# A macaron decoder block on one core: the third product ahead of two turns at the start, and the last norm's weights multiplied on GpSimd at the end

## The chip, the cores and the metric

The kernel runs on one core of one Trainium2 chip. The metric is the device time of one execution in microseconds, the median of several runs. In the rows of the profile PE is TensorE (PEld its weight loads), DVE is VectorE, ACT is ScalarE, POOL is GpSimd and SP is SyncE, which issues most DMAs.

## What is computed

One decoder block on x of 1024 tokens by 1024 channels in float32:

```
h = x + 0.5 * swiglu(rms(x, g1), w1a, w3a, w2a)      # first half-step, 2816 wide
u = rms(h, g_mix)
h = h + (sigmoid(gA) * yA + sigmoid(gB) * yB) @ W_o   # attention and pooling mixers on u
h = h + 0.5 * swiglu(rms(h, g2), w1b, w3b, w2b)      # second half-step
out = rms(h, g_final)
```

with `rms(x, g) = x / sqrt(mean(x*x) + eps) * g` and `swiglu(x, w1, w3, w2) = (silu(x @ w1) * (x @ w3)) @ w2`. The change touches the entry into the first half-step and the last norm.

## The kernel before

**Products.** Every large matrix product is cut into two by two blocks and done with seven block products in place of eight, by sums and differences of the blocks. To keep float32's accuracy with fast matmuls each operand is split into a high and a low part (`hi` and `lo`): ScalarE rounds a copy to the high part, VectorE or GpSimd subtracts it from the source for the low part, and TensorE adds up high by high, high by low and low by high. One product of a 128-wide block of weights with half the tokens (512) is thus 12 matmuls of 128x128 by 128x512 (`Sevens.product`, L316); its weights are split by ScalarE (L304, tile `wc`) and by GpSimd or VectorE (L307).

**The entry into the first half-step** (`begin_up1`, L877, an order written out by hand). The rows of x come by DMA in eight tiles of 128 tokens. TensorE runs twelve idle matmuls of ones first (`keep_on(12)`, L905), and then turns the norm's weights into a row (`gains`, L896, copied by VectorE at L912). For each tile ScalarE squares and sums (`squares`, L259), VectorE forms the mean and GpSimd takes the power (`inverse`, L263 and L264), VectorE scales half a row (L270), and TensorE turns it, 128x128 at a time, by a matmul with the identity (L392: "the turn" of a tile). ScalarE copies the turned tile as the high part (`Rows`, L393), VectorE forms the low part (`lower`, L396), and ScalarE later keeps the turned tile in h (`keep`, L400).

The low channels of tiles 0 to 3 are block b11, their high channels block b21. Products 0 to 3 of the entry multiply b11 with the first four blocks of weights (a and b of pairs 0 and 1: `u_f10a`, `u_f10b`, `u_f11a`, `u_f11b`); product 4 (`u_f10a` again) is the first that reads b21. The order on TensorE before is: product 0, turns of the high channels of tiles 0 and 1, product 1, turns of tiles 2 and 3, product 2, product 3, product 4, the turns of tile 4 (b22, then p12 by L457, then the difference t3 that GpSimd forms at L441, tile `s_f1t`), product 5, and so on (`Entry.run`, L433 on). Below, the first product is product 0, and so the third is product 2 and the fifth is product 4. ScalarE has, in this order: high parts of tiles 2 and 3, the copy of product 1 (L576), the square of tile 5, four `keep`s (L400), the operand of product 4 (L304, `wc_f10a`), the copy of product 2, the operand of product 5.

**The end.** The last products add 0.5 * (gate @ w2) into h: seven block products (`DOWN`, L97) of six steps each (`Down`, L707). A step's operands are prepared two steps ahead (`begin`): VectorE sums two blocks of weights (L766, tile `s_f2w`), ScalarE makes the high parts (L746, `bhi` and `ahi`), VectorE or GpSimd the low parts (L750, `blo` and `alo`). When a block product is complete its four banks are added into the tiles of h by VectorE (`add`, L793), and `after2(m, t)` (L2193) is called for the tile. Tiles 0 to 3 are complete after the fifth block product; their norm goes in one piece. Of tiles 4 to 7 the low channels are complete after the sixth and the high channels after the seventh:

- after the sixth, `low_half(t)` (L2154): ScalarE squares the low half and sums (L2157), writing the squares into the output tile; for tile 7 VectorE also multiplies the low halves of tiles 5 and 6 by the norm's weights (`with_gain`, L2165).
- after the seventh, `high_half(t)` (L2169), `power(t)` (VectorE L2173, GpSimd L2174), and one tile later `send_out(t)`: VectorE scales the high half by the power and the weights in one operation (L2179) and SyncE sends it; ScalarE scales the low half, which has its weights already, in place (L2183) and sends it. Tile 4's low half goes another way: `send_low(4)`, one operation of VectorE (L2189) from h, sent by SyncE.

For this last block product the last two steps are done together, tile by tile: nine matmuls for tile 4, its add and `after2`, then nine for tile 5, and so on. The operations of each engine run in the order in which the program issues them.

Of the kernel before, what the change touches and what calls it, by code (L numbers as in the profile page):

```python
# [12 lines left out]
AF = mybir.ActivationFunctionType  # L13
OP = mybir.AluOpType
AX = mybir.AxisListType

P = 128
# [109 lines left out]
def tile_block(  # L127
# [28 lines left out]
    nc = tc.nc  # L156
    ve, ac, gp, pe = nc.vector, nc.scalar, nc.gpsimd, nc.tensor
# [10 lines left out]
    def bank(tag, name):  # L168
        return psum.tile([P, HALF], F32, tag=tag, name=name)
# [18 lines left out]
    h = []  # L188
# [77 lines left out]
    def scaled(t, out, gain):  # L266
        ve.scalar_tensor_tensor(out, h[t], inv.pop(t)[:, 1:2], gain, op0=OP.mult, op1=OP.mult)
# [15 lines left out]
    LOWS, HIGHS = slice(0, HALF), slice(HALF, S)  # L283
# [575 lines left out]
    def load_all():  # L859
        load_rows(0, 1, 2, 3)  # L860
        raws.depth = 2
        raws.load()
        load_rows(4)
        raws.depth = 3
        raws.load()
        load_rows(5)
        raws.depth = 4
        raws.load()
        load_rows(6, 7)
        raws.depth = 6  # L870
        raws.load()
# [5 lines left out]
    def begin_up1():  # L877


        load_all()  # L880
        idle = bank("mm", "idle")

        def keep_on(n):

            for _ in range(n):
                pe.matmul(idle[:, :P], ones, ones, start=True, stop=True)

        def widen(b):
            k = slice(4 * b, 4 * b + 4)
            ve.tensor_copy(columns[:, k], gain1[:, k, None].to_broadcast([P, 4, P]))  # L890

        def gains(b):

            p = bank("acc", f"gain{b}")
            for k in range(4):
                pe.transpose(p[:, k * P:(k + 1) * P], columns[:, 4 * b + k], ident)  # L896
            return p

        r = {}

        def rows(t, what, c, tag="acc"):
            scaled_part(t, c, gain_row)
            r[t] = Rows(X, what, h[t][:, c], t, tag)

        keep_on(12)  # L905
        widen(0)
        squares(0, square)
        widen(1)
        inverse(0)
        g = [gains(b) for b in range(2)]  # L910
        keep_on(2)
        ve.tensor_copy(gain_row[:, LOWS], g[0])  # L912
        for t in range(1, 4):
            squares(t, square)
        inverse(1)
        rows(0, "b11", LOWS)
        keep_on(2)
        rows(1, "b11", LOWS)
        inverse(2)
        inverse(3)  # L920
        keep_on(2)
        pairs = [Pair(sv1, j, sums, True, j == 2) for j in range(3)]
        entry = pre_run(sv1, [(q, m) for m in (1, 2) for q in pairs[:2]] + [(pairs[2], m) for m in (1, 2)],
                        pairs[0], h[:4])
        entry.operand(0)
        rows(2, "b11", LOWS)
        keep_on(3)
        rows(3, "b11", LOWS, "mm")
        keep_on(2)
        ac.activation(gain_row[:, HIGHS], g[1], AF.Copy)  # L930
        for t in range(4):
            r[t].lower()
        sv1.terms = (0, 2, 1)
        entry.product(0)
        sv1.terms = (0, 1, 2)
        entry.operand(1)
        for t in range(4):
            r[t].keep(h[t][:, LOWS])

        square2 = columns_tile  # L940
        squares(4, square2)
        for t in (0, 1):
            rows(t, "b21", HIGHS)
        entry.product(1)
        entry.out(0)
        entry.operand(2)
        entry.operand(3)
        inverse(4)
        r[0].lower()
        for t in (2, 3):  # L950
            rows(t, "b21", HIGHS)
            r[t - 1].lower()
        entry.product(2)
        entry.out(1)
        squares(5, square2)
        r[3].lower()
        for t in range(4):
            r[t].keep(h[t][:, HIGHS])
        entry.product(3)
        entry.operand(4)  # L960
        entry.out(2)
        entry.operand(5)
        entry.out(3)

        def high(t, part):
            if part == 0:
                inverse(t)
                return
            scaled(t, h[t], gain_row)
            return h[t]  # L970

        def after(t):
            if t + 2 < NT:
                squares(t + 2, square2)
            if t < 6:
                raws.depth = t + 3
                raws.load()

        entry.run(high, after, 4)
        return pairs  # L980
# [304 lines left out]
    def mix_operand(k, part=0):  # L1285
        if k < len(items):
# [5 lines left out]
            else:  # L1292
# [3 lines left out]
    entry = Entry(svm, [(q.quad, m, q.out) for j in (0, 2) for m in (1, 2) for q in mixes[j:j + 2]], h[:4],  # L1296
                  mix_operand)
# [443 lines left out]
    ends = []  # L1741
# [175 lines left out]
    op = wo.enter_context(sbuf("ops", "right"))  # L1917
# [102 lines left out]
    with tc.manual_schedule():  # L2020
# [28 lines left out]
        for i in range(2, STEPS - 4):  # L2049
            step_o(i)  # L2050
            m, st = i // 2 - 1, i % 2
# [95 lines left out]
    final_gain = gains_of[1]  # L2147
# [4 lines left out]
    ends = {}  # L2152

    def low_half(t):  # L2154

        y, st = h_tile(f"n4_{t}"), small.tile([P, 4], F32, tag="nlast", name=f"nst_last{t}")
        ac.activation(y[:, LOWS], h[t][:, LOWS], AF.Square, scale=D ** -0.5, accum_out=st[:, 0:1])  # L2157
        ends[t] = y, st
        if t == 7:
            with_gain(5)  # L2160
            with_gain(6)

    def with_gain(t):
        y = ends[t][0]
        ve.tensor_tensor(y[:, LOWS], h[t][:, LOWS], final_gain[:, LOWS], op=OP.mult)  # L2165

    def high_half(t):
        y, st = ends[t]
# [7 lines left out]
    def send_out(t):  # L2176
        y, st = ends[t]
        rows = slice(t * P, (t + 1) * P)
        ve.scalar_tensor_tensor(y[:, HIGHS], h[t][:, HIGHS], st[:, 3:4], final_gain[:, HIGHS],  # L2179
                                op0=OP.mult, op1=OP.mult)  # L2180
        nc.sync.dma_start(out[rows, HIGHS], y[:, HIGHS])
        if t > 4:
            ac.activation(y[:, LOWS], y[:, LOWS], AF.Copy, scale=st[:, 3:4])  # L2183
            nc.scalar.dma_start(out[rows, LOWS], y[:, LOWS])

    def send_low(t):
        y, st = ends[t]
        rows = slice(t * P, (t + 1) * P)
        ve.scalar_tensor_tensor(y[:, LOWS], h[t][:, LOWS], st[:, 3:4], final_gain[:, LOWS],  # L2189
                                op0=OP.mult, op1=OP.mult)  # L2190
        nc.sync.dma_start(out[rows, LOWS], y[:, LOWS])

    def after2(m, t):  # L2193
        if m == len(DOWN) - 3:
            rows = slice(t * P, (t + 1) * P)
            nc.sync.dma_start(out[rows, :], norm_rows(t, final_gain, "n4", own_row))
        elif m == len(DOWN) - 2:
            low_half(4 + t)
        elif m == len(DOWN) - 1:
            high_half(4 + t)  # L2200
            if t > 0:
                send_out(3 + t)
            power(4 + t)
            if t == 0:
                with_gain(7)
            elif t == 1:
                send_low(4)
            elif t == 3:
                send_out(7)

    with sbuf("steps2", "right") as pool:
# [95 lines left out]
```

## Time and profile before

| | us |
|---|---|
| median of 3 runs (lowest, highest) | 1906.85 (1904.89, 1909.58) |
| the profiled execution | 1908.91 |
| its span, first to last instruction | 1907.0 |
| TensorE busy in it | 1888.8 |
| VectorE busy | 1328.2 |
| ScalarE busy | 774.4 |
| GpSimd busy | 713.7 |

All times in the rows are of the profiled execution, counted from the start of its span. A timeline row gives the start, the duration, the engine, the line, the operation, its tiles (output, arrow, inputs), its shape and a count where equal operations in a row are put together; in brackets stands how long the engine was idle before it and who ended that. A matmul's duration is longer than the distance to the next one, because matmuls overlap; the distance is what it costs. Releasers are inferred, and where several were waited for the name can be wrong.

### The profile page before, as it was taken

What the parts mean: (1) busy time and instruction counts of PE and PEld (TensorE: products, weight loads), DVE (VectorE), ACT (ScalarE), POOL (GpSimd) and SP (SyncE); (2) the same over time, 40 slices, a digit from 0 to 9 for tenths busy, and PEclk for the clock granted to TensorE, in tenths of its full rate; (3) what the DMA queues carried; (4) which work ended last, traced back from release to release, by engine and by line L of the source; (5) the groups of instructions that cost most, each with busy time, mean ns of one, the idle gap of its engine ahead of it and who ended that gap; (6) DMA issues with size and microseconds to landing.
All of it is one profiled execution on the core that took longest, in us unless ns stands there. A gap on an engine that the chain in (4) does not pass through costs nothing. (4 is left out here: it accounts for less than half of the span.)

```text
span 1907.0 us, 24693 instructions
## 1 busy us (share of the span) xinstructions
PE 1888.8 (99%) x8822; PEld 1564.4 (82%) x8822; DVE 1328.2 (70%) x1975; ACT 774.4 (41%) x1394; POOL 713.7 (37%) x533
## 2 busy tenths in 40 slices
PE   9999999999999999999999999999999999999998
PEld 8888888888878888888888788888888888888886
DVE  6876556558677777658886787787665566577777
ACT  7423333333335543334445762363333333333344
POOL 4433333331222354445544366543333333312131
PEclk9999999999999999999999999999999999999999
DMA  4154223336466626765578867644433223454564
GB/s 189 59 198 163 83 89 120 124 116 220 135 212 219 204 89 218 240 219 188 211 253 317 283 221 275 255 157 139 157 122 116 83 94 121 140 199 133 198 216 166
DMA packets 144020, 330.78 MB, mean 173 GB/s; under 512 B 17561, under 2 KB 39065, under 8 KB 142361
## 3 DMA queue, kind: packets, MB, share of 16 engines
q1 hardware_dynamic: 140152, 318.36, 48.2%
q10 hardware_dynamic: 3744, 10.85, 1.6%
q8 instruction: 69, 1.13, 0.2%
q14 instruction: 55, 0.44, 0.1%
HBM read 229.61 MB, written 99.55 MB: 173 GB/s over the span
## 5 line engine op out<-in xcount | busy, mean ns | idle before, releaser
L788 PE MATMUL d_f<-bhi_f,alo_f 128*128 128x512 f32 x616 | 240.3, 390 | 1.9 <-POOL alo_f L750 1.4
L788 PE MATMUL d_f<-bhi_f,ahi_f 128*128 128x512 f32 x616 | 240.4, 390 | 0.6 <-ACT h L400 0.4
L788 PE MATMUL d_f<-blo_f,ahi_f 128*128 128x512 f32 x616 | 239.7, 389 | 0.0
L750 POOL TENSOR_TENSOR alo_f<-g_f,ahi_f 128x512 fp32r<-128x512 f32 x60 | 83.4, 1407 | 276.0 <-ACT ahi_f L746 276.0
L316 PE MATMUL u_mixm<-xhi_t_mix,wc_mixm 128*128 128x512 f32 x608 | 157.7, 391 | 0.2 <-ACT wc_mixm L304 0.2
L788 PEld LDWEIGHTS d_f<-bhi_f,alo_f 128*128 128x128 f32 x616 | 115.6, 188 | 27.7 <-POOL alo_f L750 2.9
L788 PEld LDWEIGHTS d_f<-bhi_f,ahi_f 128*128 128x128 f32 x616 | 115.6, 188 | 25.1 <-ACT h L400 0.9
L788 PEld LDWEIGHTS d_f<-blo_f,ahi_f 128*128 128x128 f32 x616 | 115.6, 188 | 24.0
L316 PEld LDWEIGHTS u_mixm<-xhi_t_mix,wc_mixm 128*128 128x128 f32 x608 | 113.4, 188 | 24.1 <-ACT wc_mixm L304 0.7
L316 PE MATMUL u_mixm<-xhi_b_mix,wc_mixm 128*128 128x512 f32 x456 | 120.4, 392 | 0.5 <-DVE y_m L1068 0.5
L307 POOL TENSOR_TENSOR wc_mixm<-s_mixm,wc_mixm 128x512 fp32r<-128x512 f32 x52 | 78.0, 1501 | 110.3 <-ACT wc_mixm L304 96.2
L316 PEld LDWEIGHTS u_mixm<-xhi_b_mix,wc_mixm 128*128 128x128 f32 x456 | 84.8, 188 | 18.1 <-issue 0.9
L304 ACT ACTIVATE wc_mixm<-s_mixm 128x512 fp32r<-128x512 f32 x76 | 47.1, 629 | 110.4 <-DVE s_mixm L358 53.6
L746 ACT ACTIVATE ahi_f<-g_f 128x1024 fp32r<-128x1024 f32 x84 | 82.0, 976 | 3.6 <-DMA g_f<-gs_f 3.6
L316 PE MATMUL u_mixm<-xlo_t_mix,wc_mixm 128*128 128x512 f32 x304 | 81.3, 389 | 0.0
L307 POOL TENSOR_TENSOR wc_mixm<-raw,wc_mixm 128x512 fp32r<-128x512 f32 x40 | 59.3, 1484 | 43.1 <-ACT wc_mixm L304 32.4
L1988 PE MATMUL wo<-w_o,o_hi 128*128 128x512 f32 x224 | 69.5, 391 | 0.3 <-DVE merge L1803 0.3
L746 ACT ACTIVATE bhi_f<-s_f2w 128x512 fp32r<-128x512 f32 x55 | 32.7, 628 | 87.1 <-DVE s_f2w L766 79.4
L746 ACT ACTIVATE bhi_f<-s_f1w 128x512 fp32r<-128x512 f32 x55 | 32.7, 629 | 86.2 <-DVE s_f1w L766 72.2
L316 PEld LDWEIGHTS u_mixm<-xlo_t_mix,wc_mixm 128*128 128x128 f32 x304 | 57.1, 188 | 12.0
L750 DVE TENSOR_TENSOR alo_f<-g_f,ahi_f 128x1024 fp32r<-128x1024 f32 (+1 forms) x48 | 57.6, 1200 | 7.4 <-ACT ahi_f L746 7.4
L316 PE MATMUL u_mixm<-xlo_b_mix,wc_mixm 128*128 128x512 f32 x228 | 61.0, 389 | 0.0
(1332 smaller groups left out, 4758.6 us busy)
## 6 DMA issues: line engine op xcount, KB each, us to landing
g_f<-gs_f SPq DMA_DIRECT2D x70, 512.0 KB
gs_f<-y_f SPq DMA_DIRECT2D x88, 256.0 KB
raw<-in_w2a_dram SPq DMA_DIRECT2D x35, 512.0 KB
raw<-in_w2b_dram SPq DMA_DIRECT2D x35, 512.0 KB
gs_f<-gb_f SPq DMA_DIRECT2D x46, 256.0 KB
raw<-in_w1a_dram SPq DMA_DIRECT2D x22, 512.0 KB
raw<-in_w3a_dram SPq DMA_DIRECT2D x22, 512.0 KB
raw<-in_w1b_dram SPq DMA_DIRECT2D x22, 512.0 KB
```

Source lines behind the costliest of these rows:

```text
L304: ac.activation(w[:, 0], src, AF.Copy)
L307: eng.tensor_tensor(w[:, 1], src, w[:, 0].bitcast(F32), op=OP.subtract)
L316: pe.matmul(p, a, b, start=(start and n == 0), stop=(n == 11), skip_group_check=not start)
L746: ac.activation(hi[:, c], src, AF.Copy)
L750: eng.tensor_tensor(lo[:, d], src[:, o], hi[:, d].bitcast(F32), op=OP.subtract)
L788: pe.matmul(self.banks[m][t], l, r, start=(first and q == 0), stop=(last and q == 2))
L1988: pe.matmul(banks[m][t], l, r, start=(st == 0 and j == 0 and q == 0), stop=(st == 1 and j == 1 and q == 2))
```

## The change

Three edits. At the start the first run of idle matmuls has nine instead of twelve. Product 2 of the entry is issued ahead of the scaled rows, turns and low parts of tiles 2 and 3's high channels, directly behind product 1; the orders of VectorE, ScalarE, GpSimd and SyncE at this place stay as they were. At the end the low halves of all of tiles 4 to 7 are multiplied by the norm's weights on GpSimd, each directly behind its square, instead of tiles 5 to 7 on VectorE later; and ScalarE scales all four, so that `send_low` is gone. Tile 4's low half is still sent by SyncE, now after ScalarE has scaled it.

```diff
-        keep_on(12)
+        keep_on(9)
...
         inverse(4)
         r[0].lower()
+        entry.product(2)
         for t in (2, 3):
             rows(t, "b21", HIGHS)
             r[t - 1].lower()
-        entry.product(2)
         entry.out(1)
...
         ac.activation(y[:, LOWS], h[t][:, LOWS], AF.Square, scale=D ** -0.5, accum_out=st[:, 0:1])
         ends[t] = y, st
-        if t == 7:
-            with_gain(5)
-            with_gain(6)
-
-    def with_gain(t):
-        y = ends[t][0]
-        ve.tensor_tensor(y[:, LOWS], h[t][:, LOWS], final_gain[:, LOWS], op=OP.mult)
+        gp.tensor_tensor(y[:, LOWS], h[t][:, LOWS], final_gain[:, LOWS], op=OP.mult)
...
         nc.sync.dma_start(out[rows, HIGHS], y[:, HIGHS])
-        if t > 4:
-            ac.activation(y[:, LOWS], y[:, LOWS], AF.Copy, scale=st[:, 3:4])
-            nc.scalar.dma_start(out[rows, LOWS], y[:, LOWS])
-
-    def send_low(t):
-        y, st = ends[t]
-        rows = slice(t * P, (t + 1) * P)
-        ve.scalar_tensor_tensor(y[:, LOWS], h[t][:, LOWS], st[:, 3:4], final_gain[:, LOWS],
-                                op0=OP.mult, op1=OP.mult)
-        nc.sync.dma_start(out[rows, LOWS], y[:, LOWS])
+        ac.activation(y[:, LOWS], y[:, LOWS], AF.Copy, scale=st[:, 3:4])
+        (nc.scalar if t > 4 else nc.sync).dma_start(out[rows, LOWS], y[:, LOWS])
...
-            if t == 0:
-                with_gain(7)
-            elif t == 1:
-                send_low(4)
-            elif t == 3:
+            if t == 3:
                 send_out(7)
```

## The prediction

> **What bounds the kernel now.** I read the page first, then the timeline engine by engine around the two places that the change touches, then the chain of waits of the last 15 us.
>
> ```profile
> span 1907.0 us, 24693 instructions
> ...
> PE 1888.8 (99%) x8822; PEld 1564.4 (82%) x8822; DVE 1328.2 (70%) x1975; ACT 774.4 (41%) x1394; POOL 713.7 (37%) x533
> ```
>
> TensorE (PE) is busy 99% of the span. So nothing that another engine does counts until PE waits for it, and a wait of PE near the start is not made up later: it shifts all that follows. Only the last 10 us are different. There the chain of waits (this row sums it from 1893 us on) lies on DVE and ACT, which add the last products to h, take the norm and send the rows:
>
> ```profile
> by line: DVE h_last L793 16.2%; ACT n L2169 16.1%; ACT n L2183 13.1%; DVE n L2165 12.0%; issue 5.1%; ACTq L2184 4.6%; DVE n L2189 4.4%; DVE nst_last L2173 2.1%
> ```
>
> **Part one: three idle matmuls less.** Timeline rows (start, us, engine, line; in brackets the idle time before and who ended it):
>
> ```profile
> 1.05 5.02 PE L886 MATMUL idle<-ones 128*128 128x128 f32 x24 [1.05 <-DVE mhalf L187]
> ...
> 6.67 0.69 DVE L912 COPY gain_ffn<-gain 128x512 f32<-128x512 f32 x1 [1.09 <-PE gain L896]
> ...
> 7.10 1.06 ACT L259 ACTIVATE square<-x 128x1024 f32<-128x1024 f32 x1 [0.17 <-DMA x<-in_x_dram]
> ...
> 9.33 0.19 ACT L259 ACTIVATION_READ_ACCUMULATOR square<-x 128x1 f32 x1
> ...
> 9.55 0.15 DVE L263 TENSOR_SCALAR nst<-nst 128x1 f32<-128x1 f32 x1 [0.59 <-ACT square L259]
> ...
> 9.63 0.75 DVE L270 SCALAR_TENSOR_TENSOR x<-x,nst,gain_ffn 128x512 f32<-128x512 f32 x1
> ```
>
> Twelve idle matmuls are 24 records in 5.02 us, so three are up to 6 x 0.21 = 1.25 us. The turns of the gain come earlier by up to that, and the copy at 6.67, which waited 1.09 us for them, with them. But DVE stands in order: before tile 2's rows (9.63) it must form tile 3's mean (9.55), and that waits for ACT's fourth square, whose sum is read at 9.33 + 0.19 = 9.52. ACT's squares run on the arrival of x (the third waited for its DMA at 7.10). That cover hides the whole part: **0**. If the copy did pass its gain on, it would be worth at most the 1.09 us of its wait; I take 0, because the wait for the square is in the rows.
>
> What it can cost is the clock. The same idle matmul took 421 ns between 3 and 5 us, and 275 ns at 7 us (group rows: busy, mean ns); and later in the run a stretch in which PE was busy only 0.58 of 3 us is followed by a granted clock of 0.57 (windows: us, PE, PEld, DVE, ACT, POOL busy, PEclk):
>
> ```profile
> L886 PE MATMUL idle<-ones 128*128 128x128 f32 x11 | 2.6, 421 | 0.0
> ...
> L886 PE MATMUL idle<-ones 128*128 128x128 f32 x4 | 0.6, 275 | 0.0
> ...
> 1050.00:1053.00 3.00, 0.58 (x11) 0.38 (x9) 2.01 (x10) 1.82 (x5) 1.75 (x2) 1.00 1.01 399
> 1053.00:1057.00 4.00, 3.94 (x15) 2.90 (x16) 1.39 (x2) 3.71 (x11) 1.41 (x2) 0.57 1.02 324
> ```
>
> With nine, the idle run still reaches about 5 us and the turns follow, so I take no loss here. The Trainium skill ("TensorE: Matmul & The Clock Gate", section "Part 1: The HAM clock gate (the "warmup" mystery)") speaks against the cut: it says that the full clock comes after some 3.4 us of sustained work, in a window that runs free of the kernel's start, so that with less warm-up a run could stay slow longer. It is the fourth rival below.
>
> **Part two: the third product ahead of the turns of tiles 2 and 3.**
>
> ```profile
> 19.30 1.52 DVE L270 SCALAR_TENSOR_TENSOR x<-x,nst,gain_ffn 128x512 f32<-128x512 f32 x1
> ...
> 19.68 0.60 PE L392 MATMUL x_b<-ident,x 128*128 128x128 f32 x4
> 20.96 0.63 PE L392 MATMUL x_b<-ident,x 128*128 128x128 f32 x4 [0.68 <-ACT xhi_b_f L393]
> 21.35 1.17 PE L316 MATMUL u_f11a<-xhi_b_f,wc_f11a 128*128 128x512 f32 x4
> ...
> 24.20 1.07 PE L316 MATMUL u_f11b<-xhi_b_f,wc_f11b 128*128 128x512 f32 x4
> ...
> 26.92 1.07 PE L316 MATMUL u_f10a<-xhi_b_f,wc_f10a 128*128 128x512 f32 x4
> ...
> 30.08 0.60 PE L457 MATMUL x_b<-ident,x 128*128 128x128 f32 x4
> 30.52 0.60 PE L392 MATMUL x_t<-ident,s_f1t 128*128 128x128 f32 x4
> ```
>
> PE waits 0.68 us before tile 3's turn (20.96); DVE's scaled rows end only at 19.30 + 1.52 = 20.82. Afterwards the third product stands at 19.68 and takes what the fourth takes, 26.92 - 24.20 = 2.72 us, to 22.40. The turns follow, 0.44 each (30.52 - 30.08), at 22.40 and 22.84, now without a wait; the second ends at 22.84 + 0.60 = 23.44. The fourth product starts at 22.84 + 0.39 = 23.23 and is through 2.85 us later (21.35 to 24.20), at 26.08 instead of 26.92. So PE alone would gain 0.84. But the fifth product needs its operand from ACT, and ACT keeps its order:
>
> ```profile
> 21.63 0.60 ACT L393 ACTIVATE xhi_b_f<-x_b 128x512 fp32r<-128x512 f32 x1 [0.71 <-PE x_b L392]
> ...
> 23.64 2.06 ACT L400 ACTIVATE x<-x_b 128x512 f32<-128x512 f32 x4
> 25.55 0.67 ACT L304 ACTIVATE wc_f10a<-raw 128x512 fp32r<-128x512 f32 x1
> ...
> 26.30 1.30 POOL L307 TENSOR_TENSOR wc_f10a<-raw,wc_f10a 128x512 fp32r<-128x512 f32 x1 [3.83 <-ACT wc_f10a L304]
> ...
> 28.81 1.28 POOL L441 TENSOR_TENSOR s_f1t<-x 128x512 f32<-128x512 f32 x1
> ```
>
> Queued behind the waiting tile 3 (21.63) are the second product's copy, a square, four copies of the turned rows (23.64) and then the operand wc_f10a (25.55), end to end. From the end of tile 3's turn (20.96 + 0.63 = 21.59) to the operand's end (26.22) it is 4.63 us. Now the turn ends at 23.44, so the operand is there at 28.07 + 0.05. PE, through at 26.08, waits 2.0 us; the fifth product starts at 28.12 instead of 26.92: +1.20. A first group behind a wait takes 1.17 instead of 1.07: +0.10. GpSimd starts 0.08 after the operand and does two low parts and tile 4's difference, which ended at 28.81 + 1.28 = 30.09 and now ends at 30.09 + 1.85 = 31.94; the turn that reads it would be due at 30.52 + 1.30 = 31.82: another 0.15 to 0.2 with the signal. Then ACT, DVE and GpSimd are ahead again. **Sum +1.5 us**; ends -0.84 (ACT holds nothing up) and +2.0.
>
> **Part three: the tail.** DVE loses three multiplications L2165 and the low half of tile 4 (L2189); GpSimd gets four products of 128x512, ACT one more scaling, behind which only squares stand that wait for DVE anyway. GpSimd has nothing to do there, but it does not run beside DVE for free:
>
> ```profile
> 1860.09 1.29 DVE L267 SCALAR_TENSOR_TENSOR hn_n<-h_last,nst,gain_final 128x1024 f32<-128x1024 f32 x1 [0.66 <-POOL nst L264]
> 1861.29 1.78 DVE L750 TENSOR_TENSOR blo_f<-raw,bhi_f 128x512 fp32r<-128x512 f32 x1
> ...
> 1860.41 2.11 POOL L750 TENSOR_TENSOR alo_f<-g_f,ahi_f 128x512 fp32r<-128x512 f32 x1 [0.36 <-ACT ahi_f L746]
> ...
> 1878.59 1.28 DVE L766 TENSOR_TENSOR s_f2w<-raw,raw 128x512 f32<-128x512 f32 x2
> 1878.65 0.19 ACT L2157 ACTIVATION_READ_ACCUMULATOR n<-h_last 128x1 f32 x1
> ...
> 1883.87 1.28 DVE L766 TENSOR_TENSOR s_f2w<-raw,raw 128x512 f32<-128x512 f32 x2
> ...
> 1886.81 1.23 DVE L750 TENSOR_TENSOR alo_f<-g_f,ahi_f 128x1024 fp32r<-128x1024 f32 x1 [0.18 <-ACT ahi_f L746]
> ...
> 1889.15 0.68 DVE L766 TENSOR_TENSOR s_f2w<-raw,raw 128x512 f32<-128x512 f32 x1
> ...
> 1891.22 0.69 DVE L750 TENSOR_TENSOR alo_f<-g_f,ahi_f 128x512 fp32r<-128x512 f32 x1
> 1893.01 0.39 PE L788 MATMUL d_f<-bhi_f,alo_f 128*128 128x512 f32 x1
> ...
> 1893.02 1.29 DVE L2165 TENSOR_TENSOR n<-h_last,gain_final 128x512 f32<-128x512 f32 x2
> ```
>
> The first three rows are one collision: GpSimd came at 1860.41 while DVE ran, finished 1.14 after DVE's end (1861.38 to 1862.52), and the next DVE operation, 0.69 by itself (1891.22), took 1.78. All three read two tensors from SBUF; they take turns, first come first served. A collision costs DVE 1.78 - 0.69 = 1.1 us.
>
> The new product of tile 4 writes where ACT's square wrote, so it starts after the sum is read: 1878.65 + 0.19 + 0.08 = 1878.92. DVE is then in the first of the pair L766 (1878.59, over at about 1879.27), and the second comes only at 1879.19: GpSimd gets in between, 1.1 lost. The same pair stands behind tile 5 (1883.87): 1.1 more. Tile 6 meets the single L766 (1889.15, now 1891.35 to 1892.03): GpSimd ends at 1893.18, the low part of the last weights at 1893.73 (0.55 after it, as 1863.07 after 1862.52), alo 0.60 later at 1894.33 instead of 1891.91. The first two are covered: the operand ready at 1886.81 + 1.23 = 1888.04, now 1890.24, is first read eight matmuls of 0.227 (2.72 / 12) ahead of 1893.01, at 1891.19. The third is not: PE reads alo at 1893.01, and waits until 1894.38: **+1.4 on PE**.
>
> ```profile
> 1899.13 0.39 PE L788 MATMUL d_f<-bhi_f,alo_f 128*128 128x512 f32 x1
> ...
> 1900.15 0.69 DVE L793 SCALAR_TENSOR_TENSOR h_last<-d_f,h_last 128x512 f32<-128x512 f32 x1
> ...
> 1901.08 0.63 ACT L2169 ACTIVATE n<-h_last 128x512 f32<-128x512 f32 x1 [0.42 <-DVE h_last L793]
> ```
>
> Against that, DVE is freed: the last bank was full at 1899.52, but DVE added it only at 1900.15. With four operations of some 0.65 us less on DVE (two take 1.29 at 1893.02) the add follows PE at once: 1899.52 + 1.4 + 0.05 = 1900.97, +0.8; ACT's last square came 0.24 after the add (1900.84), behind its own DMA issue, and will come at once: -0.2. **Sum +0.6 us**; without collisions the add would be at 1899.57: -0.6 - 0.2 = -0.8; with DVE as late as before, +1.4. The Trainium skill ("SBUF — State Buffer", section "SBUF: two separate sides") gives the same exclusive turn, but has a blocked descriptor write start 115 ns after DVE's end; a product of 1.28 would then end 1.40 after DVE, 0.25 more each time, and the sum would be +1.4. The row (1.14) decides for me.
>
> **Sum.** 0 + 1.5 + 0.6 = +2.1 us on a span of 1907.0. The profiled execution took 1908.91, 2.06 above the median of the runs (1906.85); I move the median: **1909.0 us**.
>
> **Rivals.**
> 1. The faster side: ACT's queue does not hold the fifth product (this decides as soon as the operand is ready by 26.08, 2.0 us before my sum) and the tail is free of collisions: -0.84 - 0.8, 1905.2. For it: PE's wait at 20.96 does go. Against: ACT's rows run end to end. 0.10.
> 2. Only the tail is free, GpSimd slipping into DVE's gaps: 1.5 - 0.8, 1907.6. For it: DVE waits for ACT in every step (0.18 at 1886.81); against: the row at 1861.29, and that the sum of the square ends inside the pair L766 each time. 0.17.
> 3. Only the start gains: 0.6 - 0.84, 1906.6. 0.08.
> 4. The clock: a slow stretch (1053 to 1057: 0.57 of 4 us, 1.7 us lost) falls on the first products: +2.1 + 1.7, 1910.7. For it: PE then idles near 7 to 8 and 10 us; against: by my sum no gap there is over some 1 us, and at 1050 PE was idle 2.4 of 3. 0.07.
> That the change is not what it says is out: the order of instructions shows the moves.
>
> **How the numbers follow.** My forecast has 0.58. Runs of the kernel before lie between 1904.89 and 1909.58, so a median may be off by some 1.5 us. The range runs from 1905.6, most of rivals 1 to 3, to 1911.4, the upper ends and rival 4. About 0.3% (5.7 us) is what a measurement can tell from no change; all cases lie inside it: faster 0.02, same 0.93, slower 0.05.
>
> **What would show it.** After: no wait before tile 3's turn; a wait of about 2 us before the fifth product, released by ACT's wc_f10a near 28.1; DVE's second L766 at about 1.78 behind tiles 4 and 5; a PE wait of 1.4 us ahead of the last alo; the last add right behind PE. I am wrong if the fifth product starts near 26.1, or if the pair L766 keeps 1.28.

## The result and the profile after

| | before | after |
|---|---|---|
| median of 21 runs (lowest, highest), us | 1907.80 (1904.89, 1909.58) | 1910.16 (1907.49, 1912.18) |
| the profiled execution | 1908.91 | 1910.59 |
| its span | 1907.0 | 1908.8 |

The ratio is 1.0014 (95% interval 1.0009 to 1.002): 2.7 us slower, between 1.7 and 3.8, and 2.4 by the medians. Forecast were +2.1 and 1909.0, in a range of 1905.6 to 1911.4, within 0.3%. The page's head for after:

```profile
span 1908.8 us, 24680 instructions
...
PE 1890.0 (99%) x8816; PEld 1565.0 (82%) x8816; DVE 1330.1 (70%) x1971; ACT 773.6 (41%) x1395; POOL 716.5 (38%) x537
```

Only the timeline shows where the time is. TensorE in the start of after (start, us, engine, line; in brackets the idle time before and who ended it):

```profile
6.00 1.94 PE L896 MATMUL gain<-ident,columns 128*128 128x128 f32 x8 [0.74 <-DMA ident<-in_c_ident_dram]
...
19.83 1.07 PE L316 MATMUL u_f11a<-xhi_b_f,wc_f11a 128*128 128x512 f32 x4
...
22.55 1.04 PE L392 MATMUL x_b<-ident,x 128*128 128x128 f32 x8
23.35 1.17 PE L316 MATMUL u_f11b<-xhi_b_f,wc_f11b 128*128 128x512 f32 x4
...
28.32 1.20 PE L316 MATMUL u_f10a<-xhi_b_f,wc_f10a 128*128 128x512 f32 x4 [1.96 <-ACT wc_f10a L304]
...
32.18 0.66 PE L392 MATMUL x_t<-ident,s_f1t 128*128 128x128 f32 x4
```

The eight turns of tiles 2 and 3 now follow each other without a wait (22.55); in place of the 0.68 us that TensorE waited there stands 1.96 us ahead of the fifth product. The turn that reads `s_f1t` comes at 32.18 instead of 30.52. ScalarE in the same stretch is what the fifth product waits for:

```profile
23.19 1.09 ACT L393 ACTIVATE xhi_b_f<-x_b 128x512 fp32r<-128x512 f32 x2 [3.41 <-PE x_b L392]
...
25.68 2.07 ACT L400 ACTIVATE x<-x_b 128x512 f32<-128x512 f32 x4
27.59 0.68 ACT L304 ACTIVATE wc_f10a<-raw 128x512 fp32r<-128x512 f32 x1
```

Its 3.41 us of idling wait for the turns that now stand behind the third product. All that is queued behind them comes 2.0 us later than before, the operand `wc_f10a` last (27.59 instead of 25.55).

In the tail, VectorE of after:

```profile
1879.45 2.38 DVE L766 TENSOR_TENSOR s_f2w<-raw,raw 128x512 f32<-128x512 f32 x2
...
1885.82 2.38 DVE L766 TENSOR_TENSOR s_f2w<-raw,raw 128x512 f32<-128x512 f32 x2
...
1892.19 0.68 DVE L766 TENSOR_TENSOR s_f2w<-raw,raw 128x512 f32<-128x512 f32 x1
1893.65 0.90 DVE L750 TENSOR_TENSOR blo_f<-s_f2w,bhi_f 128x512 fp32r<-128x512 f32 x1 [0.78 <-ACT bhi_f L746]
...
1901.90 0.69 DVE L793 SCALAR_TENSOR_TENSOR h_last<-d_f,h_last 128x512 f32<-128x512 f32 x1 [0.40 <-PE d_f L788]
```

Both pairs L766 take 2.38 instead of 1.28 us, because a GpSimd product stands in each:

```profile
1879.77 1.52 POOL L2159 TENSOR_TENSOR n<-h_last,gain_final 128x512 f32<-128x512 f32 x1 [17.61 <-ACT n L2157]
```

And TensorE, which waited nowhere here before, waits ahead of the last step, first for ScalarE's `ahi`, which stands behind the late sum of 1892.19, and then twice more for the low parts:

```profile
1894.19 0.50 PE L788 MATMUL d_f<-bhi_f,ahi_f 128*128 128x512 f32 x1 [1.76 <-ACT ahi_f L746]
1894.61 0.51 PE L788 MATMUL d_f<-blo_f,ahi_f 128*128 128x512 f32 x1
1895.21 0.50 PE L788 MATMUL d_f<-bhi_f,alo_f 128*128 128x512 f32 x1
...
1901.48 0.39 PE L788 MATMUL d_f<-bhi_f,alo_f 128*128 128x512 f32 x1
```

So the signs that the prediction named are there, only that TensorE's wait in the tail is 2.6 us and not 1.4, and is first for `ahi`. But the sums do not close by this profile alone. TensorE is 1.72 us late at 40 us and 0.28 us **early** at 1887 us, although none of its instructions in between was changed; then it loses the 2.6 us at the end.

### The profile page after: what moved, and what is told of

It is laid out like the page before. It is cut to its first block, busy times and chain, and to the rows that moved or that the text cites. A ratio compares the mean times of both kernels' runs of the same rounds, so it can differ in the third digit from the quotient of the medians.

```text
span 1908.8 us, 24680 instructions
## 1 busy us (share of the span) xinstructions
PE 1890.0 (99%) x8816; PEld 1565.0 (82%) x8816; DVE 1330.1 (70%) x1971; ACT 773.6 (41%) x1395; POOL 716.5 (38%) x537
## 4 chain that ended last, share of the span: by engine, by line
PE 39%; DVE 4%; DMA 2%; issue 2%; ACT 2%; POOL 1%; ACTq 0%; SPq 0%; POOLq 0%; DVEq 0%
PE d_f L788 7%; PE wo L1988 3%; PE yp L1735 2%; PE u_mixm L316 1%; PE ya L1801 1%; PE o L1676 1%; PE u_f20b L316 1%; PE u_f21a L316 1%; PE u_f210a L316 1%; PE u_f29b L316 1%; PE u_f29a L316 1%; PE u_f28b L316 1%; PE u_f28a L316 1%; PE u_f27b L316 1%; PE u_f27a L316 1%
## 5 line engine op out<-in xcount | busy, mean ns | idle before, releaser
L788 PE MATMUL d_f<-bhi_f,ahi_f 128*128 128x512 f32 x616 | 240.4, 390 | 2.2 <-ACT ahi_f L746 1.8
L788 PE MATMUL d_f<-bhi_f,alo_f 128*128 128x512 f32 x616 | 240.3, 390 | 1.4 <-POOL alo_f L750 0.9
L788 PE MATMUL d_f<-blo_f,ahi_f 128*128 128x512 f32 x616 | 239.8, 389 | 0.0
L788 PEld LDWEIGHTS d_f<-bhi_f,alo_f 128*128 128x128 f32 x616 | 115.6, 188 | 27.7 <-POOL alo_f L750 2.4
L788 PEld LDWEIGHTS d_f<-bhi_f,ahi_f 128*128 128x128 f32 x616 | 115.6, 188 | 26.5 <-ACT ahi_f L746 2.2
L788 PEld LDWEIGHTS d_f<-blo_f,ahi_f 128*128 128x128 f32 x616 | 115.6, 188 | 24.2 <-DVE blo_f L750 0.2
```

What stands on the lines that cost most here:

```text
L788: pe.matmul(self.banks[m][t], l, r, start=(first and q == 0), stop=(last and q == 2))
```

## A way to read all runs: start, middle, tail

The experiments were made to find out whether the start's loss is really given back in between. For each profile I took two instructions: the first matmul of `u_f12a`, the first product behind the part of the entry that the change touches (40.53 us before), and the 53rd-last matmul of L788, ahead of the tail (1887.34 us before). They cut the span into start, middle and tail. TensorE has no changed instruction in the middle of any of these kernels (the changed tail's first GpSimd products fall into its last 8 us). The column "end chain" is explained below the table. The time is the median of 11 or 12 runs (21 for after), the ratio is against the kernel before on the same chip, less one, in per mille with its 95% interval.

| kernel | start | middle | tail | end chain | span | time less before, medians | ratio - 1, per mille |
|---|---|---|---|---|---|---|---|
| before | 40.53 | 1846.81 | 19.63 | 37.75 | 1906.97 | | |
| after | 42.25 | 1844.82 | 21.74 | 38.72 | 1908.81 | +2.36 | 1.4 (0.9 to 2.0) |
| e13, after again | 44.60 | 1843.39 | 20.72 | 38.74 | 1908.70 | +2.64 | 1.2 (0.3 to 2.1) |
| e1, part two | 42.14 | 1843.44 | 19.44 | 37.72 | 1905.02 | -0.43 | 0.3 (-0.5 to 1.2) |
| e12, parts one and two | 42.31 | 1844.95 | 19.32 | 37.72 | 1906.59 | +1.77 | 0.9 (0.0 to 1.8) |
| e3, part one | 40.60 | 1842.13 | 19.37 | 37.72 | 1902.09 | -1.17 | -0.9 (-1.8 to 0.0) |
| e8, start late | 41.49 | 1844.30 | 20.32 | 37.72 | 1906.11 | -0.34 | 0.1 (-0.8 to 1.0) |
| e9, fourth product thrice | 45.97 | 1844.64 | 20.48 | 37.75 | 1911.09 | +3.02 | 2.1 (1.2 to 3.0) |
| e2, part three | 40.78 | 1842.92 | 20.68 | 38.75 | 1904.38 | +0.62 | 0.7 (-0.1 to 1.6) |
| e7, products on VectorE | 40.64 | 1843.57 | 21.25 | 38.85 | 1905.46 | +1.87 | 1.5 (0.6 to 2.3) |
| e4, products moved | 40.44 | 1845.28 | 21.71 | 39.46 | 1907.43 | +1.34 | 0.6 (-0.3 to 1.5) |
| e6, start and tail moved | 39.99 | 1844.72 | 21.43 | 39.46 | 1906.14 | +0.59 | 0.7 (-0.2 to 1.6) |
| e10, products held back | 41.02 | 1844.14 | 19.16 | 37.34 | 1904.32 | -0.88 | -0.4 (-1.2 to 0.5) |
| e11, best of these | 40.90 | 1842.92 | 19.35 | 37.55 | 1903.17 | -1.47 | -1.1 (-2.0 to -0.2) |

The middle differs by 4.7 us between profiles, and not by the start: it is 1842.9 us in e2, whose start is 0.25 late, and 1844.6 in e9, whose start is 5.44 late. The profile of before happens to have the longest middle of all. That is why after looked as if it had been given something back: of the 13 others, every one has "gained" between 1.5 and 4.7 us on it. A profile is one execution, and executions of one kernel differ as much (before: 1904.89 to 1909.58); the profiled one is the shortest of 11 in e2 and e7 and the longest in e9, so the column "span" is no measure of a kernel.

Matmul by matmul, the 14 profiles differ in two places of the middle: by 2.4 us between 560 and 572 us of before, and by 3.0 us between 1045 and 1059. No other place gives more than 0.8. From 41 to 440 us every profile keeps the lateness of its start to 0.1 us, e9 its 5.44 us too. In the two places e9 and e4, whose start is on time, agree to 0.2 us.

The column "tail" is no measure of its part either. In the six kernels with the old tail (before, e1, e12, e3, e8, e9) TensorE's last 53 matmuls stand within 11.79 to 11.81 us, but the last add comes 0.72 to 1.85 us behind the last of them, and the tail lies between 19.32 and 20.48. VectorE waits for TensorE nowhere in it. The last thing from outside that VectorE waits for is a transfer of weights, 38 us ahead of the end. Before, and then after:

```profile
1869.22 1.29 DVE L766 TENSOR_TENSOR s_f2w<-raw,raw 128x512 f32<-128x512 f32 x2 [0.30 <-DMA raw<-in_w2b_dram]
```

```profile
1870.08 1.29 DVE L766 TENSOR_TENSOR s_f2w<-raw,raw 128x512 f32<-128x512 f32 x2 [0.65 <-DMA raw<-in_w2b_dram]
```

From this sum to the end of the span, the end chain of the table, it is 37.72 to 37.75 us in all six, and 38.72 to 38.75 in the three with the changed tail (after, e13, e2). So the changed tail costs 1.0 us. That TensorE loses 2.6 us in after and 1.56 in e2 only shows how far it had been ahead of VectorE. With the start's 1.72 the sum is 2.7, as measured by the ratio.

## Experiments on the start

### e1: part two alone

```diff
         r[0].lower()
+        entry.product(2)
         for t in (2, 3):
             rows(t, "b21", HIGHS)
             r[t - 1].lower()
-        entry.product(2)
```

> The kernel before with part two alone: the third product is issued ahead of the turns of tiles 2 and 3; 12 idle products and the old tail. In the start both theories say the same: the fifth product starts about 2 us behind the end of the fourth, released by ScalarE's wc_f10a, and the sixth product near 32.4 instead of 30.875 us (+1.5). Theory A (the forecast: a wait near the start is not made up) says +1.5 us on the whole, between +1.3 and +1.8. Theory B (later stalls give it back: the changed kernel's profile had the sixth product at +1.72, the product near 460 us at +1.5, the one near 996 at +0.6 and the one near 1053 at 0.0) says under +1.0, near +0.5.

The start is 1.61 us late, as both theories said. The time (ratio 1.0003, interval 0.9995 to 1.0012, so -1.0 to +2.3 us) cannot tell the theories apart: by the ratio it is +0.6, as theory B has it, by the medians -0.4, below both, and a dose of 1.6 us is no larger than the interval.

### e8: a pure delay

```diff
-        keep_on(12)
+        keep_on(20)
```

> The kernel before with 20 idle products instead of 12 ahead of the turns of the norm's weights: 16 more matmul rows of 0.1115 us at full clock move these turns from 6.006 to 7.69 us, a pure delay of 1.69 us at the start, with nothing else changed. Theory A (a delay at the start is carried to the end): +1.5 to +1.7 us. Theory B (later stalls give it back): under +1.0, near +0.5, with TensorE's products near 1053 us at the same time as before.

The dose was smaller than meant. The turns came 1.10 and `u_f12a` 0.96 us later, because more of the idle matmuls were short (284 ns mean between 4 and 7 us, against 421 between 3 and 5 in before). 1.0001 (0.9992 to 1.001) is as open as e1. Two inconclusive runs called for a larger dose.

### e9: three times the delay

```diff
+        sv1.terms = (0, 1, 2) * 3
         entry.product(3)
+        sv1.terms = (0, 1, 2)
```

with `start` and `stop` of each twelve matmuls as for a product of its own.

> The kernel before, whose fourth product in the start is computed three times into its bank, each time from the beginning, so that the last one counts: 24 more matmuls of 0.2267 us, 5.44 us of TensorE, less the 0.9 us for which TensorE waits ahead of the fifth product anyway: +4.5 us at the fifth product, a dose three times that of the third product's place. Theory A (a delay in the start is carried to the end): +4.2 to +4.8 us. Theory B (later stalls give back what they can, some 1.5 us as in the runs so far): +2.5 to +3.5. If later stalls give back all of it, under +1.

TensorE in e9:

```profile
31.47 1.07 PE L316 MATMUL u_f11b<-xhi_b_f,wc_f11b 128*128 128x512 f32 x4
32.38 1.07 PE L316 MATMUL u_f10a<-xhi_b_f,wc_f10a 128*128 128x512 f32 x4
```

The fifth product comes at 32.38 instead of 26.92, 5.46 late and not 4.5: the expectation counted a wait of 0.9 us that the kernel before does not have there (26.92 follows the group of 24.20 at 0.227 us a matmul). The time is 1.0021 (1.0012 to 1.003), +4.0 us between +2.3 and +5.7; +3.0 by medians. That rules out that later stalls give back all of a start delay, the reading that after's profile had suggested; it does not rule out that they keep a part of it: of 5.44 us 1.4 by the ratio and 2.4 by the medians, whose +3.0 lies in theory B's range (+2.5 to +3.5). By the table, the middle of e9 is as long as that of kernels whose start is on time.

### e3: part one alone

```diff
-        keep_on(12)
+        keep_on(9)
```

> The kernel before with part one alone: 9 idle products instead of 12. Theory A (the forecast): the turns of the norm's weights start at 6.0 us either way, so 0.0, between -0.1 and +0.1. Rival (the clock): the 0.74 us without a matmul ahead of these turns keeps the granted clock at half past them, as in the changed kernel's profile (matmuls of 0.421 us up to 9.5 us, first product at 13.345 instead of 12.970): +0.15 to +0.4.

The turns start at the same time (6.13 against 6.01 us), and `u_f12a` is 0.07 late: by the start, the forecast's zero holds. The time is 1.7 us lower (interval -3.4 to 0.0), which neither theory has. Its middle is the shortest of all (1842.13), and nothing in the start shows a gain. I take it for a draw, for e12 has the same edit and no gain; but no run here proves that, and one profile's middle does not explain the median of 11 runs.

What part one can cost shows in the grouped rows of the same turns, between 5.9 and 9 us (busy, mean ns of one). After:

```profile
L896 PE MATMUL gain<-ident,columns 128*128 128x128 f32 x8 | 1.9, 424 | 0.7 <-DMA ident<-in_c_ident_dram 0.7
```

and e3, with the same nine idle products:

```profile
L896 PE MATMUL gain<-ident,columns 128*128 128x128 f32 x8 | 1.1, 276 | 0.9 <-DMA ident<-in_c_ident_dram 0.9
```

In both TensorE idles 0.7 to 0.9 us ahead of the turns, for the identity's DMA; once the turns then take 424 ns each, once 276. (The granted clock is given as 1.00 between 5 and 9 us in both; only the durations tell.) This is no rare draw: in the five profiles with nine idle products the turns take 424 ns in four (after, e11, e12, e13) and 276 in e3; in the nine with twelve or more, 272 to 278 in eight and 322 in e10. The first product came 0.38 us late in after, 0.11 in e3, 0.44 in e12, 1.04 in e11 and 1.09 in e13 (mean 0.6); in the seven profiles with twelve idle products (e1, e2, e4, e6, e7, e9, e10) between -0.04 and 0.53, mean 0.2. The rule cited in the prediction from the Trainium skill ("TensorE: Matmul & The Clock Gate", section "Part 1: The HAM clock gate (the "warmup" mystery)"), a window that runs free of the kernel's start, fits these two rows: the same instructions at the same time, 424 and 276 ns.

### e12 and e13: the start's two parts, and the whole change again

e12 is the kernel before with the first two edits and the old tail; e13 is the changed kernel itself.

```diff
-        keep_on(12)
+        keep_on(9)
...
         r[0].lower()
+        entry.product(2)
         for t in (2, 3):
             rows(t, "b21", HIGHS)
             r[t - 1].lower()
-        entry.product(2)
```

> Parts one and two together, with the old tail. Theory A (the forecast for the start): +1.5 us. Theory B (later stalls give most of it back; 5.42 us of delay came out as +3.0, 1.0 us as +0.2): 0 to +0.8. If 9 idle products alone were worth -1.7: -1.0 to 0.0. The changed kernel of the same call less this one is the tail's price.

> The changed kernel itself once more, beside its parts on the same chip: +2.4 us again (forecast +2.1); less the run of parts one and two it gives the tail's price: +0.6 to +0.7 by the forecast, +1.0 to +1.4 by the tail alone as it ran, +1.8 or more if the start's shift leaves VectorE no lead into the last steps, as in the changed kernel's profile.

e12 is 1.0009 (1.0 to 1.0018): +1.5 by the mean of its runs, +1.8 by medians, on a start 1.78 us late. This fits a start's loss that reaches the end, as forecast, though the interval of 0 to 3.4 us is wide and touches zero. e13 gives +2.3 (0.6 to 4.0), so the tail in company costs 0.9 us by the medians (1910.18 - 1909.31), and 1.0 by the end chains (38.74 - 37.72).

The profile of e13 also shows a second price of the same wait. TensorE:

```profile
29.27 1.19 PE L316 MATMUL u_f10a<-xhi_b_f,wc_f10a 128*128 128x512 f32 x4 [1.99 <-ACT wc_f10a L304]
30.31 1.62 PE L316 MATMUL u_f10a<-xlo_b_f,wc_f10a 128*128 128x512 f32 x4
31.73 1.91 PE L316 MATMUL u_f10a<-xhi_b_f,wc_f10a 128*128 128x512 f32 x4
```

and its windows (us, PE busy, PEclk, DMA share, GB/s):

```profile
27.00:30.60 3.60, 1.61 (x8) 1.00 0.00 0
30.60:34.00 3.40, 3.40 (x11) 0.50 0.00 0
```

After a stretch in which TensorE was busy 1.61 of 3.60 us, the granted clock is 0.50 for 3.4 us, from 1.3 us behind the start of the fifth product on. That product stands 0.95 us behind after's (29.27 against 28.32; its first product was late already), the sixth 2.37 (34.96 against 32.59): the drop cost 1.4. After and e12 (1.96 us) and e1 (1.99 us) have the same wait and no such drop.

### e6: the wait taken away

```diff
         inverse(4)
         r[0].lower()
+        entry.product(2)
...
-        entry.product(2)
         entry.out(1)
+        entry.operand(4)
+        entry.operand(5)
         squares(5, square2)
...
         entry.product(3)
-        entry.operand(4)
         entry.out(2)
-        entry.operand(5)
```

and the tail of e4, below.

> The third product ahead of the turns of tiles 2 and 3, but with the operands of the fifth and sixth product (wc_f10a, wc_f10b on ScalarE and GpSimd) issued ahead of tile 5's square and the four keeps, and the tail of the run before with free GpSimd products; 12 idle products. In the start the fifth product starts near 26.3 instead of 26.9 us and the sixth near 29.9 to 30.2 instead of 30.875 (-0.7 to -1.0), if ScalarE's queue is what held the fifth product. Theory A (a gain in the start is carried): -1.3 to -1.8 us with the tail's -0.7. Theory B (later stalls take it): -0.6 to -0.9, from the tail alone. If GpSimd's collisions with VectorE hold the operands instead, no gain in the start.

TensorE of e6, and then ScalarE:

```profile
25.17 1.07 PE L316 MATMUL u_f11b<-xhi_b_f,wc_f11b 128*128 128x512 f32 x4
26.08 1.07 PE L316 MATMUL u_f10a<-xhi_b_f,wc_f10a 128*128 128x512 f32 x4
...
29.92 0.66 PE L392 MATMUL x_t<-ident,s_f1t 128*128 128x128 f32 x4
```

```profile
24.56 0.64 ACT L304 ACTIVATE wc_f10a<-raw 128x512 fp32r<-128x512 f32 x1
```

With the operand taken out of the queue behind the square and the four copies, the fifth product follows the fourth at once (26.08; 28.32 in after). The 0.84 us that TensorE alone was to gain are there (26.08 against 26.92), and 0.60 of them are left at the turn that reads `s_f1t` (29.92 against 30.52). So ScalarE's order was the cause, and the moved product is worth something only together with it. The whole kernel gained nothing (1.0007, 0.9998 to 1.0016): by the profile its tail took it, with an end chain of 39.46 us, 1.7 longer than the old one.

## Experiments on the tail

### e2: part three alone

The tail of the change on the kernel before (its diff is the third edit above).

> The kernel before with part three alone: the tail's four lower products on GpSimd, all scaled by ScalarE; the start as before. Both theories: the second L766 row behind tiles 4 and 5 takes 1.78 instead of 0.68 us, and the last step's blo and alo rows come about 2.4 us later than before. Theory A (the forecast): of that 0.95 us is slack of TensorE, 0.6 is given back at the last add and 0.2 behind it, so +0.6 to +0.7 us. Theory B (the tail carries most of the change's +2.4 us, since VectorE sets the pace of the last steps already): +1.4 to +1.9, with the last alo products 2.0 us or more later than before.

VectorE of e2:

```profile
1875.01 2.38 DVE L766 TENSOR_TENSOR s_f2w<-raw,raw 128x512 f32<-128x512 f32 x2
...
1897.47 0.69 DVE L793 SCALAR_TENSOR_TENSOR h_last<-d_f,h_last 128x512 f32<-128x512 f32 x1 [0.40 <-PE d_f L788]
```

The pair takes 2.38 again. The end chain is 38.75 us, 1.0 longer than with the old tail, as in after and e13: between the two theories (0.6 to 0.7, 1.4 to 1.9). By runs it is 1.0007 (0.9999 to 1.0016), +1.3 us, and +0.6 by the medians, which cannot tell them apart. TensorE loses 1.56 us there (forecast 1.4).

### e7: the same place, another engine

Against the changed tail, with the start of before:

```diff
-        gp.tensor_tensor(y[:, LOWS], h[t][:, LOWS], final_gain[:, LOWS], op=OP.mult)
+        ve.tensor_tensor(y[:, LOWS], h[t][:, LOWS], final_gain[:, LOWS], op=OP.mult)
```

> The changed tail alone, with the four lower products on VectorE at the place where the change has GpSimd's: each takes 0.60 us in VectorE's queue ahead of or behind the L766 sums instead of holding one of them for 1.10 us. Forecast: three products make the last blo and alo rows 1.8 instead of 2.4 us late, TensorE waits 0.85 instead of 1.5 us, and with 0.8 given back at and behind the last add the end is at 0.0 to +0.2 us, about 0.5 to 0.9 ahead of the run with GpSimd. If GpSimd's collisions are not the cost: +0.7 to +1.3 as with GpSimd.

VectorE of e7:

```profile
1874.80 1.28 DVE L793 SCALAR_TENSOR_TENSOR h_last<-d_f,h_last 128x512 f32<-128x512 f32 x2
1876.28 0.69 DVE L2159 TENSOR_TENSOR n<-h_last,gain_final 128x512 f32<-128x512 f32 x1 [0.20 <-ACT n L2157]
1876.89 1.29 DVE L766 TENSOR_TENSOR s_f2w<-raw,raw 128x512 f32<-128x512 f32 x2
```

The pair L766 has its 1.29 us back, but the time is 1.0015 (1.0006 to 1.0023), no better than with GpSimd; the expectation of 0.0 to +0.2 failed. It had left out that the product waits for ScalarE's square (0.20 us idle) at the head of VectorE's queue: a step is 0.89 us longer instead of 0.60 (from 1874.80 to the next L793 pair at 1880.97 are 6.17 us, before 5.28). GpSimd's collision costs 1.09, but VectorE pays in three steps: its last `alo` is 2.7 us late along the end chain, with GpSimd, whose third product only meets a low part, 2.4. The end chains are 38.85 and 38.75. So the price is mainly that of the place, ahead of the sums that the last steps need, and only a little that of the engine.

### e4: a later place in the program that is no later start

```diff
+        if t == 7:
+            with_gain(4)
+            with_gain(5)
...
+            if t < 2:
+                with_gain(6 + t)
```

with `with_gain` on GpSimd in place of the product behind each square.

> The kernel before with the tail on GpSimd and ScalarE as in the change, but with the four GpSimd products issued where VectorE has no sum of weights left: those of tiles 4 and 5 behind the last lower square, 6 and 7 behind the first two powers. If the tail's cost is that the products meet the L766 sums (forecast, +1.4 at TensorE), TensorE no longer waits in the last steps, the last add stands right behind the last matmul (0.43 instead of 1.03 us) and the end is 0.6 to 0.8 us ahead of the kernel before, 1.6 to 2.0 us ahead of the run with the changed tail alone. If the tail is slow for another reason (four ScalarE scalings, SyncE's queue), it stays at +0.7 to +1.3.

GpSimd of e4:

```profile
1877.66 1.51 POOL L2165 TENSOR_TENSOR n<-h_last,gain_final 128x512 f32<-128x512 f32 x1 [16.77 <-ACT n L2157]
1884.03 1.51 POOL L2165 TENSOR_TENSOR n<-h_last,gain_final 128x512 f32<-128x512 f32 x1 [4.86 <-ACT n L2157]
```

The products of tiles 4 and 5 started where they had started before, directly behind their squares: GpSimd had nothing else in its queue, and a place further down the program holds nothing back. The collisions stayed, and the products of tiles 6 and 7 now met VectorE's last scalings (L2179 at 1.78 instead of 0.75 us). The expected gain didn't come: 1.0006 (0.9997 to 1.0015), an end chain of 39.46 us, 1.7 longer than with the old tail. The edit failed; the idea behind it was not yet tested.

### e10: held back by data

Against the kernel before:

```diff
-        ac.activation(y[:, LOWS], h[t][:, LOWS], AF.Square, scale=D ** -0.5, accum_out=st[:, 0:1])
         ends[t] = y, st
+        spare = ends[4][0] if t == 7 else y
+        ac.activation(spare[:, LOWS], h[t][:, LOWS], AF.Square, scale=D ** -0.5, accum_out=st[:, 0:1])
         if t == 7:
-            with_gain(5)
-            with_gain(6)
+            with_gain(4, gp)
+            with_gain(5, gp)
+            with_gain(6, ve)
```

Tile 7's product stays on VectorE behind the first power; ScalarE scales all four.

> The kernel before with a tail in which nothing stands between the last adds and the L766 sums: the last lower square (tile 7) writes its unused squares into tile 4's row, so that GpSimd's product of tile 4, and tile 5's behind it, wait for it; the products of tiles 6 and 7 are VectorE's, in the old places; ScalarE scales all four rows. If the place ahead of the sums is the tail's cost: no TensorE wait in the last steps, VectorE's steps keep 5.28 us, the last add stands 0.43 instead of 1.03 us behind the last matmul, and the time is 0.4 to 0.8 us under the kernel before. If ScalarE's fourth scaling or the output queues are the cost: +0.5 to +1.0, with no TensorE wait.

GpSimd, then VectorE of e10:

```profile
1891.15 2.71 POOL L2167 TENSOR_TENSOR n<-h_last,gain_final 128x512 f32<-128x512 f32 x2 [30.83 <-ACT n L2159]
```

```profile
1876.34 1.28 DVE L766 TENSOR_TENSOR s_f2w<-raw,raw 128x512 f32<-128x512 f32 x2
...
1881.62 1.28 DVE L766 TENSOR_TENSOR s_f2w<-raw,raw 128x512 f32<-128x512 f32 x2
...
1891.37 0.68 DVE L793 SCALAR_TENSOR_TENSOR h_last<-d_f,h_last 128x512 f32<-128x512 f32 x1
...
1897.50 0.68 DVE L793 SCALAR_TENSOR_TENSOR h_last<-d_f,h_last 128x512 f32<-128x512 f32 x1
```

The products wait for the last square, the pairs keep 1.28 us and their distance of 5.28, TensorE waits nowhere, and the last add stands 0.56 us behind the last matmul of 1896.94. The end chain is 37.34 us, 0.4 shorter than with the old tail and 1.4 shorter than e2's; the time -0.8 us (-2.3 to +1.0), no clear gain. As ScalarE scales all four as in the change, neither the fourth scaling nor the output queues are the cost.

### e11: the best of these

e6's start, e10's tail, and nine idle products.

```diff
-        keep_on(12)
+        keep_on(9)
...
+        entry.operand(4)
+        entry.operand(5)
         squares(5, square2)
...
+            with_gain(4, gp)
+            with_gain(5, gp)
+            with_gain(6, ve)
```

> 9 idle products, the third product ahead of the turns with the operands of the fifth and sixth ahead of the square and the keeps (sixth product 0.5 us earlier than in the kernel before), and the tail of the run before. Theory A: 0.0 from the idle products, -0.5 from the start, -0.6 from the tail: -1.1 us. If the -1.7 us measured with 9 idle products alone were real: -2.0 to -2.8. Theory B (the start's gain is taken later): -0.4 to -0.8.

Measured is 0.9989 (0.998 to 0.9998): -2.1 us by the ratio, between -3.8 and -0.4, and -1.5 by medians: faster than both kernels. In its profile the first product is 1.04 us late (the turns of the norm's weights took 424 ns), and the repaired order takes that down to 0.37 at `u_f12a`; the end chain is 37.55 us. So the gain that its profile can place is the end chain's 0.2, less than the start's loss, and where the rest comes from stays open. The measured size fits theory A's -1.1 and the sum with e3's gain alike, and doesn't settle e3.

## Why the prediction was right, and which terms were off

- **Part one, 0.** The turns did not come earlier: right, though by another cover than the one named; they wait for the identity's DMA (6.00, idle 0.74), ahead of any square. The clock was not free: 0.15 us of after's shift were there before the third product (19.83 against 19.68). The step that "the turns follow" the idle run failed: 0.74 us lie between them, and the turns then took 424 ns. This is the fourth rival's mechanism at a tenth of its price of 1.7. In e13 it cost nearly that (1.4), but behind part two's own wait.
- **Part two, +1.5.** Every step stands: third product 19.83 (19.68), turns 22.55 (22.40), fourth product 23.35 (23.23), operand's end 27.59 + 0.68 = 28.27 (28.07), fifth product 28.32 (28.12), the turn of `s_f1t` +1.66, less the 0.15 it came in with +1.5. e6 shows the cause by taking it away.
- **"A wait of PE near the start is not made up later."** After's own profile seemed to refute it. The profiles keep the start's lateness to 0.1 us from 41 to 440 us. In the time, start losses of 0.96 (e8), 1.61 (e1), 1.78 (e12) and 5.44 us (e9) came out as 0.2, 0.6, 1.7 and 4.0 by the ratios, each with some 1.7 us to either side: all below the loss, none clearly. So it holds in the main, and a part given back is not ruled out.
- **Part three, +0.6.** The collisions were right: each pair lost 1.10 us, and the last `alo` starts 24.4 us behind the sum that heads the end chain instead of 22.0, 2.4 late as forecast. The wait was put at `alo`; TensorE waits for ScalarE's `ahi` first (1.76 us in after). Along the end chain the last add stands 0.9 us later (31.82 instead of 30.93), forecast was 0.8. The mis-sized term is the -0.2 behind the add. The last DMA of ScalarE's queue is indeed issued 0.2 us sooner behind it (3.23 against 3.44), but then the closing instructions take 0.3 longer: +0.1. So the tail is +1.0 in after, e13 and e2 alike, instead of +0.6. The prediction also let VectorE and ScalarE set only the last 10 us; by the end chain it is the last 38.

  The step that "PE reads alo at 1893.01, and waits until 1894.38: +1.4" measured 1.56 in e2 and 1.60 in e13, and 2.63 in after. In after the operands entered the tail with 1.1 us less lead on TensorE than in before: its `alo` of 1877.11 was 0.86 late while TensorE was 0.28 early. Of the 0.86, 0.52 came from a transfer, as ScalarE's rows show, before and then after:

```profile
1866.60 1.06 ACT L746 ACTIVATE ahi_f<-g_f 128x1024 fp32r<-128x1024 f32 x1 [1.65 <-DMA g_f<-gs_f]
```

```profile
1867.12 1.06 ACT L746 ACTIVATE ahi_f<-g_f 128x1024 fp32r<-128x1024 f32 x1 [2.54 <-DMA g_f<-gs_f]
```

  The rest came from the weights ahead of the end chain (1870.08 against 1869.22, idle 0.65 against 0.30).
- The sum, +2.1, was thus close to 2.4 or 2.7 with its largest term right and the tail 0.4 us short. That the total came out so near is in part luck: no run gives the time of a part to better than some 1.7 us to either side. Of the 1.2 us between 1909.0 and 1910.16, 0.95 is the starting point, the median of before of 3 runs (1906.85) against 21 (1907.80). The rule of the Trainium skill ("SBUF — State Buffer", section "SBUF: two separate sides") weighed there gave +1.4 for the tail by a longer collision. The collisions did not bear that out: the pair lost 1.10 us (2.38 - 1.28), as in the row of 1.78 that was used.

Open: the 1.7 us of e3 and the size of e11's gain; what sets the length of the two places in the middle; and whether a part of a start delay is kept on the way (5.44 us came out as +2.3 to +5.7).

## What to carry to other kernels

Moving work ahead on the busiest engine gains nothing if the engine that feeds the next step keeps its old order: move the operand with the product, or the wait only changes its place. In a tail, ask for each added operation what the last steps still need from the engines and the memory it uses, and hold it back by a data dependency, since its place in the program does not delay it on an idle engine. An engine that is 99% busy need not set the end: look for the last wait on a transfer and what hangs on it. And never take one profile's shift in an unchanged stretch for something given back: compare that stretch over several kernels first.

## What the runs showed of the hardware that was not expected

- The unchanged middle varied by 4.7 us over 14 profiles. The largest part sits between 1045 and 1059 us, where the DMA share is 1.0: before is shown in the prediction (a granted clock of 0.57 after the wait); in e3 (us, PE busy, PEclk, DMA share, GB/s) TensorE waited less, in two pieces, and the clock stayed up:

```profile
1045.00:1049.00 4.00, 3.25 (x27) 1.00 1.02 411
1049.00:1053.00 4.00, 3.04 (x17) 1.00 1.08 348
1053.00:1057.00 4.00, 4.00 (x35) 1.00 0.97 370
```

- A TensorE wait of 2 us can cost 1.4 us more behind it: 3.4 us at a granted clock of 0.50 in e13, none in after, e1 and e12 with the same wait.
- An operation of GpSimd on two SBUF tensors that arrives while VectorE runs such a one took 1.51 us, and VectorE's next 1.78. A VectorE operation that reads PSUM was not slowed: L793 at 1891.37 in e10 takes 0.68 us within a GpSimd row of two products from 1891.15 to 1893.86.
- The end of the kernel repeats to 0.03 us once the last weights are there (37.72 to 37.75 us in six profiles), while the 1.9 ms ahead of it vary by microseconds.
